# A decoder step on one Trainium2 core: two heads of the recurrent mixer share each level product

## The chip, the cores and the metric

One core of a Trainium2 chip runs the whole program. The metric is the device time of one execution in microseconds; the time before is a median of 2497.12 us over three runs.

## The reference

The program is one inference step of a two-layer decoder for a prompt of 1024 tokens and, with the same weights, for 8 sample tokens. Layer 0 mixes tokens with a gated linear recurrence (4 heads, a 128x128 state each) beside a memory attention; layer 1 with stick-breaking attention beside a memory attention; each layer ends in a SwiGLU FFN. The change concerns the recurrence of the prompt alone:

```python
b = jnp.cumsum(fi, axis=2)
o_inter = jnp.einsum('bhtk,bhkv->bhtv', qi * jnp.exp(b), S)
rel = b[:, :, :, None, :] - b[:, :, None, :, :]
dec = jnp.exp(jnp.where(causal, rel, -jnp.inf))
att = jnp.einsum('bhtk,bhsk,bhtsk->bhts', qi, ki, dec)
o = o_inter + jnp.einsum('bhts,bhsv->bhtv', att, vi)
```

The score of a query t and an earlier key s is a product over 128 features in which each feature has decayed by its own forget factors between s and t.

## The kernel before

The prompt is worked on in two halves of 512 tokens, g = 0 and g = 1; the sample's 8 tokens ride as columns 512 to 519 of the second half. Activations are feature-major: 128 features on the partitions, tokens along the columns. Weight products (`proj`, L274) split each fp32 weight into two parts (ACT L260, DVE L261) and multiply three times. The file is a set of generators; `weave` draws from several in turn, and the tile framework's scheduler then writes out a fixed order for each engine, by priority and by modelled times, so pieces of one generator may move past those of another. Engines wait for each other by semaphores, in order.

The recurrence of one half is `hgrn_prompt`. Its inputs, one pair of heads (`hp`) to a tile of [128, 2, 520], are forget factors F, keys K and queries Q from `gate_proj` and `heads2`, and the values V, token-major, from `v_proj`. For chunks of 128 tokens it builds the decayed score matrix `atts[h]` by doubling:

- The diagonal first: K times Q (L1160), masked by the identity (L1162); then Q is multiplied by F (L1167).
- Seven levels, m = 1, 2, ..., 64. A block of 2m tokens has an early and a late half of m tokens. All keys of a chunk are the stationary operand and the late queries the 64 moving columns (L1180): 8 fp32 matmuls for a pair of heads. Then DVE brings operands to the next level: late queries times the early half's total decay (L1185), early keys times the late half's total decay (L1186), and the totals of the halves multiplied (L1187). The block scores, early keys against late queries, go from PSUM into `atts` under a byte mask (L1190). One yield for each level and pair.
- Each head's end: keys turned (L1201), states (L1207, L1220), outputs from scores and values (L1215) and from the state carried in (L1219), and a norm (L303, L1226, L1228).

Score tiles and other temporaries come from pool `B` (7 buffers), level products from `S` (3 PSUM banks).

Where it stands in the order of the program:

- Setup: byte masks, two POOL selections (L163, L166) and one DVE cast (L169) each; rows of x are normed (L366 to L371), transposed (L396) and split (L399, L400).
- g = 0: `rows_proj` makes the values (L1048; its PSUM is copied out at L1054 and L1055), then gates and queries (`fq`), then the recurrence woven with the memory keys and values: `mem_keys` (L812, L817 to L822) and `mem_values` (L839).
- g = 1: gates and queries are woven with the memory attention of g = 0, the values with the end of the output projection, the recurrence with the first part of the FFN of g = 0 (`f0.part(0)`: L274 with L291 to L295 and L703).

Of the kernel before, what the change touches and what calls it, by code (L numbers as in the profile page):

```python
# [18 lines left out]
P = 128  # L19
# [5 lines left out]
def tile_decoder(  # L25
# [46 lines left out]
    def nm(s):  # L72
        uid[0] += 1
        return f"{s}_{uid[0]}"
# [62 lines left out]
    make_identity(nc, ident)  # L137
    ones = const.tile([P, P], F32, name="ones")
    nc.vector.memset(ones, 1.0)
    epsb = const.tile([P, 1], F32, name="epsb")  # L140
    nc.vector.memset(epsb, EPS)
    trif = const.tile([P, P], F32, name="trif")
# [11 lines left out]
        compare_op=ALU.is_equal, fill=0.0, base=0, channel_multiplier=0,  # L154
    )

    mask = const.tile([P, 7, 64], U8, name="mask")
    for lv in range(7):
        m = 1 << lv
        nb = 64 // m  # L160
        mf = tpool.tile([P, nb, m], F32, tag="t", name=nm("mf"))
        src = ones[:, 0:64].rearrange("p (b m) -> p b m", m=m)
        nc.gpsimd.affine_select(  # L163
            mf, src, pattern=[[-2 * m, nb], [0, m]], compare_op=ALU.is_ge, fill=0.0, base=0, channel_multiplier=1
        )
        nc.gpsimd.affine_select(  # L166
            mf, mf, pattern=[[2 * m, nb], [0, m]], compare_op=ALU.is_ge, fill=0.0, base=m - 1, channel_multiplier=-1
        )
        nc.vector.tensor_copy(mask[:, lv, :], mf.rearrange("p b m -> p (b m)"))  # L169

    xsraw = const.tile([P, ND, NB], F32, name="xsraw")
    par = const.tile([P, P], F32, name="par")
# [107 lines left out]
    def split_to(dst, src):  # L280
        nc.scalar.copy(dst[0], src)  # L281
        nc.vector.tensor_sub(dst[1], src, dst[0].bitcast(F32))  # L282

    def silu(dst, ps, g):

# [771 lines left out]
    def v_proj(g, W, m0, xt, vt, vs):  # L1057
        vt.extend((C(), C()) if g else (A(), A()))
        if not g:
            yield from rows_proj(W, m0, xt, vt)  # L1060
            return
        for h in range(H):
            ps = proj(g, W, 0, ND, m0 + h * P, xt)
            t = T()
            nc.scalar.copy(sv(t, g), pv(ps, g))
            to_token(t, vt, h)
            if g:
                nc.vector.tensor_copy(vs[:, h, :], t[:, G : G + NB])
            yield

    def gate_proj(g, W, xt, Ft, Kt):
        n = NG[g]
        for h in range(H):
            if h % 2 == 0:
                Ft.append(A())
                Kt.append(A())
            ps = proj(g, W, 0, ND, 4 * P + h * P, xt)
            f = T()
            nc.scalar.copy(sv(f, g), pv(ps, g))
            e = T()  # L1080
# [72 lines left out]
    def hgrn_prompt(g, Ft, Kt, Qt, Vt):  # L1153
        atts = []
        for h in range(H):
            K_, Q_ = Kt[h // 2][:, h % 2, :], Qt[h // 2][:, h % 2, :]
            pd = S()
            for c in range(CH):
                cs = slice(c * P, (c + 1) * P)
                nc.tensor.matmul(pd[:, cs], K_[:, cs], Q_[:, cs], start=True, stop=True)  # L1160
            at = B()
            nc.vector.tensor_mul(  # L1162
                at.rearrange("p (c t) -> p c t", c=CH), pd.rearrange("p (c t) -> p c t", c=CH),
                ident.unsqueeze(1).to_broadcast([P, CH, P]),
            )
            atts.append(at)
            nc.vector.tensor_mul(Q_[:, :G], Q_[:, :G], Ft[h // 2][:, h % 2, :G])  # L1167
            yield
        for lv in range(7):
            m = 1 << lv  # L1170
            nbg = G // (2 * m)
            for hp in range(2):
                F_, K_, Q_ = Ft[hp], Kt[hp], Qt[hp]
                pl = S()
                plv = pl.rearrange("p (h c n) -> p h c n", h=2, c=CH)
                for hh in range(2):
                    for c in range(CH):
                        cs = slice(c * P, (c + 1) * P)
                        rhs = Q_[:, hh, cs].rearrange("p (b t m) -> p b t m", t=2, m=m)[:, :, 1, :]
                        nc.tensor.matmul(plv[:, hh, c, :], K_[:, hh, cs], rhs, start=True, stop=True)  # L1180
                for hh in range(2):
                    Qv = Q_[:, hh, :G].rearrange("p (b t m) -> p b t m", t=2, m=m)
                    Kv = K_[:, hh, :G].rearrange("p (b t m) -> p b t m", t=2, m=m)
                    Fv = F_[:, hh, :G].rearrange("p (b t m) -> p b t m", t=2, m=m)
                    nc.vector.tensor_mul(Qv[:, :, 1, :], Qv[:, :, 1, :], Fv[:, :, 0, 0:1].to_broadcast([P, nbg, m]))  # L1185
                    nc.vector.tensor_mul(Kv[:, :, 0, :], Kv[:, :, 0, :], Fv[:, :, 1, 0:1].to_broadcast([P, nbg, m]))  # L1186
                    nc.vector.tensor_mul(Fv[:, :, 0, 0:1], Fv[:, :, 0, 0:1], Fv[:, :, 1, 0:1])  # L1187
                nb = 64 // m
                for hh in range(2):
                    nc.vector.copy_predicated(  # L1190
                        atts[hp * 2 + hh].rearrange("p (c b t m) -> p c b t m", c=CH, t=2, m=m)[:, :, :, 1, :],
                        mask[:, lv, :].rearrange("p (b m) -> p b m", m=m).unsqueeze(1).to_broadcast([P, CH, nb, m]),
                        pl[:, hh * 256 : (hh + 1) * 256].rearrange("p (c b m) -> p c b m", c=CH, m=m),
                    )
                yield
        for h in range(H):
            F_, K_, Q_ = Ft[h // 2][:, h % 2, :], Kt[h // 2][:, h % 2, :], Qt[h // 2][:, h % 2, :]
            pk = S()
            for c in range(CH):
                cs = slice(c * P, (c + 1) * P)  # L1200
                nc.tensor.transpose(pk[:, cs], K_[:, cs], ident)  # L1201
            kT = B()
            nc.scalar.copy(kT, pk)
            pd = S()
            for c in range(CH):
                cs = slice(c * P, (c + 1) * P)
# [3 lines left out]
            for c in range(CH):  # L1210
                cs = slice(c * P, (c + 1) * P)
                has = not (g == 0 and c == 0)
                cur = carry[:, h, :] if c == 0 else Sa[:, (c - 1) * P : c * P]
                nxt = carry[:, h, :] if c == CH - 1 else Sa[:, cs]
# [19 lines left out]
    class mixer_a:  # L1234
# [5 lines left out]

        def fq(self):
            yield from gate_proj(self.g, self.W, self.xt, self.F, self.K)
            yield from heads2(self.g, self.W, 0, self.xt, silu, A, self.Q)

        def v(self):
            yield from v_proj(self.g, self.W, 8 * P, self.xt, self.V, self.vs)
# [312 lines left out]
```

## Time and profile before

| | us |
|---|---|
| runs shown | 2499.96, 2497.12, 2493.58 |
| median | 2497.12 |
| the profiled execution | 2499.1 |
| its span, first to last instruction | 2497.4 |
| PE busy | 2462.8 |
| PEld (weight loads) busy | 2169.9 |
| DVE busy | 1571.8 |
| ACT busy | 1183.0 |
| POOL busy | 98.3 |

The granted TensorE clock is 0.997 over the span. The page gives busy time by engine and the chain of work that ended last; the trace can be asked for windows of time, for single lines of the code, for the instructions in order of time, and for waits. In a row of the timeline stand start and length in microseconds, the engine, the line, the operation, output and inputs, their sizes and the number of instructions; in brackets the idle time before it and what ended that. An fp32 matmul appears as two instructions.

### The profile page before, as it was taken

Reading aid. Unit: us, or ns where it says so; the run is one execution under the profiler, and the core shown is the slowest. Engines: PE = TensorE matmul, PEld = TensorE weight load, DVE = VectorE, ACT = ScalarE, POOL = GpSimd, SP = SyncE. Lnnn points to the kernel's source line nnn. Section 1 sums busy time; section 2 is a strip of 40 time slices with the busy share of each in tenths; the row PEclk is TensorE's granted clock in tenths of the full one; section 3 lists DMA queues with packets and bytes.
Section 4 is the critical chain, followed back from the end, with each engine's and each line's share of the span. In section 5 each row is a group of like instructions: output and inputs, shape, how many; then the busy total and the mean of one; then the engine's idle time right before and its main releaser. Section 6 shows DMA issues by size and latency. Waiting matters only on the chain.

```text
span 2497.4 us, 40764 instructions
## 1 busy us (share of the span) xinstructions
PE 2462.8 (99%) x15565; PEld 2169.9 (87%) x15565; DVE 1571.8 (63%) x2756; ACT 1183.0 (47%) x2277; POOL 98.3 (4%) x139
## 2 busy tenths in 40 slices
PE   8999999999999999999999999999999999999998
PEld 6888988877877897999999989877787797999997
DVE  5766556655765585655544575777577648755655
ACT  5446543243433454555433454555444445564444
POOL 1000000000000000010111100022000000000000
PEclk9999999999999999999999999999999999999999
DMA  5352252233643447586678976544454234365542
GB/s 186 114 165 68 72 156 81 60 110 116 184 124 98 129 138 227 156 195 177 173 191 215 234 193 196 160 142 138 121 149 130 85 115 122 121 192 145 151 137 69
DMA packets 496110, 358.21 MB, mean 143 GB/s; under 512 B 19110, under 2 KB 443635, under 8 KB 495915
## 3 DMA queue, kind: packets, MB, share of 16 engines
q1 hardware_dynamic: 477354, 301.08, 40.5%
q0 software_dynamic: 18560, 54.53, 9.1%
q8 instruction: 122, 2.00, 0.3%
q14 instruction: 74, 0.60, 0.1%
HBM read 325.73 MB, written 75.94 MB: 161 GB/s over the span
## 4 chain that ended last, share of the span: by engine, by line
PE 88%; DVE 5%; DMA 3%; ACT 2%; issue 2%; POOL 0%; SPq 0%; DVEq 0%; ACTq 0%; POOLq 0%
PE mm L274 59%; PE q L552 7%; PE q L667 5%; PE s L1180 2%; PE q L510 2%; PE mm L1048 2%; PE s L903 1%; PE s L862 1%; PE mm L812 1%; DMA b<-qd 1%; PE mm L839 1%; DVE ws L261 1%; PE ns L957 1%; PE s L1336 1%; DMA c<-in_cache_sb_v,pidx 1%
## 5 line engine op out<-in xcount | busy, mean ns | idle before, releaser
L274 PE MATMUL mm<-x,ws 128*128 128x260 f32 (+1 forms) x7776 | 1332.9, 330 | 0.0
L274 PEld LDWEIGHTS mm<-x,ws 128*128 128x128 f32 x7776 | 1148.3, 188 | 151.5 <-issue 12.0
L260 ACT CAST ws<-w 128x512 fp32r<-128x512 f32 x712 | 420.2, 591 | 763.2 <-PE mm L274 620.2
L261 DVE TENSOR_TENSOR ws<-w,ws 128x512 fp32r<-128x512 f32 x712 | 462.5, 653 | 286.8 <-ACT ws L260 278.3
L274 PE MATMUL mm<-m,ws 128*128 128x512 f32 (+1 forms) x2112 | 393.5, 343 | 0.1
L274 PEld LDWEIGHTS mm<-m,ws 128*128 128x128 f32 x2112 | 324.4, 189 | 49.9 <-issue 2.6
L667 PE MATMUL q<-m,ws 128*128 128x260 f32 x1056 | 128.8, 283 | 0.0
L667 PEld LDWEIGHTS q<-m,ws 128*128 128x128 f32 x1056 | 127.2, 188 | 0.4 <-ACT hT L485 0.2
L543 DVE TENSOR_TENSOR ws<-w,ws 128x512 fp32r<-128x512 f32 x126 | 86.6, 691 | 61.5 <-ACT ws L542 59.3
L552 PE MATMUL q<-y,ws 128*128 128x260 f32 x864 | 112.9, 283 | 0.0
L542 ACT CAST ws<-w 128x512 fp32r<-128x512 f32 x126 | 78.0, 621 | 69.6 <-PE q L667 27.4
L552 PEld LDWEIGHTS q<-y,ws 128*128 128x128 f32 x864 | 107.6, 189 | 0.0
L291 DVE TENSOR_SCALAR t<-mm 128x512 f32<-128x512 f32 (+1 forms) x82 | 56.7, 692 | 79.6 <-PE mm L274 79.6
L447 DVE TENSOR_TENSOR r<-r,mm 128x512 f32<-128x512 f32 (+1 forms) x96 | 66.0, 688 | 61.1 <-PE mm L274 60.3
L703 DVE TENSOR_TENSOR t<-t,mm 128x512 f32<-128x512 f32 (+1 forms) x66 | 45.5, 690 | 74.2 <-PE mm L274 73.9
L295 DVE TENSOR_TENSOR t<-t,t 128x512 f32<-128x512 f32 (+1 forms) x66 | 45.8, 694 | 70.6 <-ACT t L294 70.6
L552 PE MATMUL q<-x,ws 128*128 128x260 f32 x648 | 86.3, 282 | 0.0
L552 PEld LDWEIGHTS q<-x,ws 128*128 128x128 f32 x648 | 81.3, 188 | 0.0
L314 DVE TENSOR_TENSOR st<-st,n 128x512 f32<-128x512 f32 (+1 forms) x98 | 67.1, 691 | 8.8 <-ACT n L313 7.0
L281 ACT CAST m<-t 128x512 fp32r<-128x512 f32 (+1 forms) x88 | 54.9, 624 | 18.1 <-DVE t L703 8.9
L282 DVE TENSOR_TENSOR m<-t,m 128x512 fp32r<-128x512 f32 (+1 forms) x88 | 61.0, 693 | 2.6 <-ACT m L281 1.4
L984 POOL DMA_INDIRECT c<-in_cache_sb_k,pidx x16 | 16.4, 1026 | 1170.5 <-ACT n L313 958.6
(339 smaller groups left out, 2557.9 us busy)
## 6 DMA issues: line engine op xcount, KB each, us to landing
w<-in_w_gu SPq DMA_DIRECT2D x334, 256.0 KB, 3.4
w<-in_w_down SPq DMA_DIRECT2D x160, 256.0 KB, 3.5
w<-in_w_in_a SPq DMA_DIRECT2D x80, 256.0 KB, 3.0
wsum<-in_w_gu POOLq DMA_DIRECT2D x18, 1024.0 KB, 9.5
w<-wsum SPq DMA_DIRECT2D x72, 256.0 KB, 3.8
w<-in_w_o SPq DMA_DIRECT2D x64, 256.0 KB, 2.8
wsum<-in_w_gu POOLq DMA_DIRECT2D x12, 1280.0 KB, 10.7
w<-in_w_mem_kv SPq DMA_DIRECT2D x32, 256.0 KB, 3.2
```

Source lines behind the costliest of these rows:

```text
L260: nc.scalar.copy(ws[:, 0, :n, :], raw[:, :n, :])
L261: nc.vector.tensor_sub(ws[:, 1, :n, :], raw[:, :n, :], ws[:, 0, :n, :].bitcast(F32))
L274: nc.tensor.matmul(ps[:, a, : PW[g]], wt, xt[k][:, xi, o : o + PW[g]], start=(k == 0 and wi == 0), stop=(k == nk - 1 and wi == 2),)
L281: nc.scalar.copy(dst[0], src)
L282: nc.vector.tensor_sub(dst[1], src, dst[0].bitcast(F32))
L291: nc.vector.tensor_scalar(sv(x, g), pv(ps, g), -44.0, None, op0=ALU.max)
L314: nc.vector.tensor_add(acc[:, :n], acc[:, :n], t[:, :n])
L447: nc.vector.tensor_add(dst, dst, pv(ps, g))
L542: nc.scalar.copy(w[:, 0, :], src)
L543: nc.vector.tensor_sub(w[:, 1, :], src, w[:, 0, :].bitcast(F32))
L552: nc.tensor.matmul(ps[:, :h], w[:, wj, k * P : (k + 1) * P], x[:, xi, :], start=(first and k == 0 and wi == 0), stop=(k == 3 and wi == 2), ...
L667: nc.tensor.matmul(pp[a][:, :h], wt, mids[k][:, xi, a * h : (a + 1) * h], start=(k == 0 and wi == 0), stop=(k == nf - 1 and wi == 2),)
```

## The change

Two heads of a pair share each level product. The odd heads' tokens are stored back to front in time, so that where the even head's late halves are odd blocks, the odd head's are even blocks. A combined key matrix takes the even blocks of the even head and the odd blocks of the odd head (the early halves of each); it meets, as one moving operand of 128 columns, the late queries of both heads. Half of each product's rows belong to the wrong head and are left out by the masks, which now exist for both sides.

- In `hgrn_prompt` three storage places, x (the combined keys), y (the other blocks) and z (next level's x), take turns; `move` brings them from one level to the next: an ACT copy of blocks from y to z, a DVE scaling from x to z, a DVE scaling from x to y. A first `move` builds x, with one more yield. z is a tile from `B`.
- Query scalings and totals are one DVE instruction for the pair.
- `put` and `rev` write odd heads reversed in `gate_proj` and in the new `silu_heads`, with the 8 sample columns apart. The values of odd heads are reversed with a flip matrix on PE in the first half and by a reversed ACT write in the second. The chunks of odd heads are walked backwards, and their output is written reversed.

```diff
+    flip = const.tile([P, P], F32, name="flip")
+    nc.gpsimd.affine_select(
+        flip, ones, pattern=[[1, P]], compare_op=ALU.is_equal, fill=0.0, base=1 - P, channel_multiplier=1
+    )
...
+        for side in range(2):
+            o = side * m
...
+            nc.vector.tensor_copy(mask[:, lv, side, :], mf.rearrange("p b m -> p (b m)"))
...
+    def rev(ap):
+        st, n = ap.ap[-1]
+        return bass.AP(ap.tensor, ap.offset + (n - 1) * st, [list(d) for d in ap.ap[:-1]] + [[-st, n]])
+
+    def put(dst, src, h, g, op):
+        n = NG[g]
+        if h % 2 == 0:
+            op(dst[:, :n], src[:, :n])
+            return
+        op(dst[:, :G], rev(src[:, :G]))
+        if g:
+            op(dst[:, G:n], src[:, G:n])
...
+    def silu_heads(dst, ps, g, h):
...
+        put(dst, x, h, g, lambda o, i: nc.scalar.activation(o, i, AF.Exp, scale=-1.0))
+        nc.scalar.activation(d, d, AF.Ln, bias=1.0)
+        nc.scalar.activation(d, d, AF.Exp, scale=-1.0)
+        put(dst, x, h, g, lambda o, i: nc.vector.tensor_mul(o, o, i))
...
+            odd = [t[:, :, :512].rearrange("p c (e o d) -> p c e o d", o=2, d=P)[:, :, :, 1] for t in vt]
+            pts = [S(), S()]
+            for c in range(CH):
+                r = CH - 1 - c
+                nc.tensor.matmul(
+                    pts[c // 2][:, (c % 2) * 256 : (c % 2) * 256 + 256], flip, odd[r // 2][:, r % 2],
+                    start=True, stop=True,
+                )
+            for i in range(2):
+                pt = pts[i].rearrange("p (c e d) -> p c e d", c=2, d=P)
+                for c in range(2):
+                    nc.any.tensor_copy(odd[i][:, c], pt[:, c])
...
-            nc.scalar.activation(Fd, e[:, :n], AF.Exp)
-            nc.scalar.activation(Kd, f[:, :n], AF.Exp)
+            put(Fd, e, h, g, lambda o, i: nc.scalar.activation(o, i, AF.Exp))
+            put(Kd, f, h, g, lambda o, i: nc.scalar.activation(o, i, AF.Exp))
...
+        def view(t, o, *dims):
+            return bass.AP(t.tensor, t.offset + o, [list(t.ap[0])] + [list(d) for d in dims])
+
+        def move(F_, x, y, z, m):
+            if m == 0:
+                keep, swap, fk = [0, [2, G // 2]], [1, [2, G // 2]], None
+            elif m == 64:
+                keep, swap = [0, [P, CH], [1, m]], [m, [P, CH], [1, m]]
+                fk, fs = [m, [P, CH], [0, m]], [WID, [P, CH], [0, m]]
+            else:
+                nq = G // (4 * m)
+                keep, swap = [0, [4 * m, nq], [3 * m, 2], [1, m]], [m, [4 * m, nq], [m, 2], [1, m]]
+                fk = [m, [4 * m, nq], [WID + m, 2], [0, m]]
+                fs = [WID, [4 * m, nq], [3 * m - WID, 2], [0, m]]
+            nc.scalar.copy(view(z, *swap), view(y, *swap))
+            if fk is None:
+                nc.vector.tensor_copy(view(z, *keep), view(x, *keep))
+                nc.vector.tensor_copy(view(y, *swap), view(x, *swap))
+                return
+            nc.vector.tensor_mul(view(z, *keep), view(x, *keep), view(F_, *fk))
+            nc.vector.tensor_mul(view(y, *swap), view(x, *swap), view(F_, *fs))
+
+        xs, zs = [Kt[hp][:, 0, :G] for hp in range(2)], [B() for _ in range(2)]
+        for hp in range(2):
+            move(Ft[hp], xs[hp], Kt[hp][:, 1, :G], zs[hp], 0)
+            xs[hp], zs[hp] = zs[hp][:, :], xs[hp]
+        yield
...
-                plv = pl.rearrange("p (h c n) -> p h c n", h=2, c=CH)
-                for hh in range(2):
-                    for c in range(CH):
-                        cs = slice(c * P, (c + 1) * P)
-                        rhs = Q_[:, hh, cs].rearrange("p (b t m) -> p b t m", t=2, m=m)[:, :, 1, :]
-                        nc.tensor.matmul(plv[:, hh, c, :], K_[:, hh, cs], rhs, start=True, stop=True)
...
-                    nc.vector.tensor_mul(Qv[:, :, 1, :], Qv[:, :, 1, :], Fv[:, :, 0, 0:1].to_broadcast([P, nbg, m]))
-                    nc.vector.tensor_mul(Kv[:, :, 0, :], Kv[:, :, 0, :], Fv[:, :, 1, 0:1].to_broadcast([P, nbg, m]))
-                    nc.vector.tensor_mul(Fv[:, :, 0, 0:1], Fv[:, :, 0, 0:1], Fv[:, :, 1, 0:1])
...
+                for c in range(CH):
+                    o = c * P
+                    nc.tensor.matmul(
+                        pl[:, o : o + P], x[:, o : o + P],
+                        view(Q_, o + m, [WID - m, 2], [2 * m, nb], [1, m]), start=True, stop=True,
+                    )
+                late = view(Q_, m, [WID - m, 2], [2 * m, nbg], [1, m])
+                nc.vector.tensor_mul(late, late, view(F_, 0, [WID + m, 2], [2 * m, nbg], [0, m]))
+                move(F_, x, Kt[hp][:, 1, :G], z, m)
+                xs[hp], zs[hp] = z, x
+                first = F_[:, :, :G].rearrange("p h (b t m) -> p h b t m", t=2, m=m)
+                nc.vector.tensor_mul(first[:, :, :, 0, 0], first[:, :, :, 0, 0], first[:, :, :, 1, 0])
...
+                c = CH - 1 - i if h % 2 else i
...
-            nc.vector.scalar_tensor_tensor(F_[:, :G], po, hgn, r, op0=ALU.mult, op1=ALU.mult)
+            o = F_[:, :G]
+            if h % 2:
+                o = rev(o)
+            nc.vector.scalar_tensor_tensor(o, po, hgn, r[:, :G], op0=ALU.mult, op1=ALU.mult)
```

More of the change, by code (lines that the diff above doesn't have):

```diff
@@ L155, in tile_decoder @@
     )
-    mask = const.tile([P, 7, 64], U8, name="mask")
+    mask = const.tile([P, 7, 2, 64], U8, name="mask")
     for lv in range(7):
@@ L160, in tile_decoder @@
         nb = 64 // m
[L161 to L169, printed above, removed]
+        for side in range(2):
+            o = side * m
+            mf = tpool.tile([P, nb, m], F32, tag="t", name=nm("mf"))
+            src = ones[:, 0:64].rearrange("p (b m) -> p b m", m=m)
+            nc.gpsimd.affine_select(
+                mf, src, pattern=[[-2 * m, nb], [0, m]], compare_op=ALU.is_ge, fill=0.0, base=-o,
+                channel_multiplier=1,
+            )
+            nc.gpsimd.affine_select(
+                mf, mf, pattern=[[2 * m, nb], [0, m]], compare_op=ALU.is_ge, fill=0.0, base=o + m - 1,
+                channel_multiplier=-1,
+            )
+            nc.vector.tensor_copy(mask[:, lv, side, :], mf.rearrange("p b m -> p (b m)"))
     xsraw = const.tile([P, ND, NB], F32, name="xsraw")
@@ L282, in split_to @@
         nc.vector.tensor_sub(dst[1], src, dst[0].bitcast(F32))
+    def rev(ap):
[10 more added lines that the diff above has]
+    def silu_heads(dst, ps, g, h):
+        n = NG[g]
+        x = T()
+        d = dst[:, :n]
+        nc.vector.tensor_scalar(sv(x, g), pv(ps, g), -44.0, None, op0=ALU.max)
+        put(dst, x, h, g, lambda o, i: nc.scalar.activation(o, i, AF.Exp, scale=-1.0))
+        nc.scalar.activation(d, d, AF.Ln, bias=1.0)
+        nc.scalar.activation(d, d, AF.Exp, scale=-1.0)
+        put(dst, x, h, g, lambda o, i: nc.vector.tensor_mul(o, o, i))
     def silu(dst, ps, g):
@@ L1060, in v_proj @@
             yield from rows_proj(W, m0, xt, vt)
+            odd = [t[:, :, :512].rearrange("p c (e o d) -> p c e o d", o=2, d=P)[:, :, :, 1] for t in vt]
[5 more added lines that the diff above has]
+                    start=True, stop=True,
+                )
+            for i in range(2):
[3 more added lines that the diff above has]
+            yield
             return
@@ L1064, in v_proj @@
             t = T()
[L1065 to L1068, printed above, removed]
+            n = NG[g]
+            if h % 2:
+                o = rev(t[:, :n].rearrange("p (a n) -> p a n", a=2))
+                o = bass.AP(o.tensor, o.offset + n // 2, [list(o.ap[0]), [-(n // 2), 2], list(o.ap[2])])
+                nc.scalar.copy(o, pv(ps, g))
+                to_token(t[:, NB:n], vt, h)
+                nc.vector.tensor_copy(vs[:, h, :], rev(t[:, :NB]))
+            else:
+                nc.scalar.copy(sv(t, g), pv(ps, g))
+                to_token(t, vt, h)
+                nc.vector.tensor_copy(vs[:, h, :], t[:, G:n])
             yield
@@ L1168, in hgrn_prompt @@
             yield
+        def view(t, o, *dims):
[6 more added lines that the diff above has]
+                fk, fs = [m, [P, CH], [0, m]], [WID, [P, CH], [0, m]]
+            else:
+                nq = G // (4 * m)
[9 more added lines that the diff above has]
+            nc.vector.tensor_mul(view(y, *swap), view(x, *swap), view(F_, *fs))
@@ L1169, in hgrn_prompt @@
+        xs, zs = [Kt[hp][:, 0, :G] for hp in range(2)], [B() for _ in range(2)]
+        for hp in range(2):
+            move(Ft[hp], xs[hp], Kt[hp][:, 1, :G], zs[hp], 0)
+            xs[hp], zs[hp] = zs[hp][:, :], xs[hp]
+        yield
         for lv in range(7):
             m = 1 << lv
-            nbg = G // (2 * m)
+            nb, nbg = 64 // m, G // (2 * m)
             for hp in range(2):
-                F_, K_, Q_ = Ft[hp], Kt[hp], Qt[hp]
+                F_, Q_ = Ft[hp][:, :, :], Qt[hp][:, :, :]
+                x, z = xs[hp], zs[hp]
@@ L1174, in hgrn_prompt @@
                 pl = S()
-                plv = pl.rearrange("p (h c n) -> p h c n", h=2, c=CH)
-                for hh in range(2):
-                    for c in range(CH):
-                        cs = slice(c * P, (c + 1) * P)
-                        rhs = Q_[:, hh, cs].rearrange("p (b t m) -> p b t m", t=2, m=m)[:, :, 1, :]
[L1180 to L1187, printed above, removed]
@@ L1188, in hgrn_prompt @@
-                nb = 64 // m
+                for c in range(CH):
[3 more added lines that the diff above has]
+                        view(Q_, o + m, [WID - m, 2], [2 * m, nb], [1, m]), start=True, stop=True,
+                    )
+                late = view(Q_, m, [WID - m, 2], [2 * m, nbg], [1, m])
+                nc.vector.tensor_mul(late, late, view(F_, 0, [WID + m, 2], [2 * m, nbg], [0, m]))
+                move(F_, x, Kt[hp][:, 1, :G], z, m)
@@ L1193, in hgrn_prompt @@
-                        pl[:, hh * 256 : (hh + 1) * 256].rearrange("p (c b m) -> p c b m", c=CH, m=m),
+                        atts[hp * 2 + hh].rearrange("p (c b t m) -> p c b t m", c=CH, t=2, m=m)[:, :, :, 1 - hh, :],
+                        mask[:, lv, hh, :].rearrange("p (b m) -> p b m", m=m).unsqueeze(1).to_broadcast([P, CH, nb, m]),
+                        pl.rearrange("p (c h b m) -> p c h b m", c=CH, h=2, m=m)[:, :, hh],
                     )
@@ L1209, in hgrn_prompt @@
             po = S()
-            for c in range(CH):
+            for i in range(CH):
+                c = CH - 1 - i if h % 2 else i
                 cs = slice(c * P, (c + 1) * P)
-                has = not (g == 0 and c == 0)
-                cur = carry[:, h, :] if c == 0 else Sa[:, (c - 1) * P : c * P]
-                nxt = carry[:, h, :] if c == CH - 1 else Sa[:, cs]
+                has = not (g == 0 and i == 0)
+                cur = carry[:, h, :] if i == 0 else Sa[:, (i - 1) * P : i * P]
+                nxt = carry[:, h, :] if i == CH - 1 else Sa[:, i * P : (i + 1) * P]
                 nc.tensor.matmul(
@@ L1227, in hgrn_prompt @@
             r = rstd_from(osq, G, 1.0 / P, kT, S)
-            nc.vector.scalar_tensor_tensor(F_[:, :G], po, hgn, r, op0=ALU.mult, op1=ALU.mult)
+            o = F_[:, :G]
+            if h % 2:
+                o = rev(o)
+            nc.vector.scalar_tensor_tensor(o, po, hgn, r[:, :G], op0=ALU.mult, op1=ALU.mult)
             yield
@@ L1242, in fq @@
             yield from gate_proj(self.g, self.W, self.xt, self.F, self.K)
-            yield from heads2(self.g, self.W, 0, self.xt, silu, A, self.Q)
+            for h in range(H):
+                if h % 2 == 0:
+                    self.Q.append(A())
+                ps = proj(self.g, self.W, 0, ND, h * P, self.xt)
+                silu_heads(self.Q[-1][:, h % 2, :], ps, self.g, h)
+                yield
         def v(self):
```

2 lines of the change are left out of this document (removed).

## The prediction

> **What bounds the kernel now.** First the page: the summary of the engines and the chain of work that ended last.
>
> ```profile
> span 2497.4 us, 40764 instructions
> PE 2462.8 (99%) x15565; PEld 2169.9 (87%) x15565; DVE 1571.8 (63%) x2756; ACT 1183.0 (47%) x2277; POOL 98.3 (4%) x139
> ...
> PE 88%; DVE 5%; DMA 3%; ACT 2%; issue 2%; POOL 0%; SPq 0%; DVEq 0%; ACTq 0%; POOLq 0%
> PE mm L274 59%; PE q L552 7%; PE q L667 5%; PE s L1180 2%; PE q L510 2%; PE mm L1048 2%; PE s L903 1%; PE s L862 1%; PE mm L812 1%; DMA b<-qd 1%; PE mm L839 1%; DVE ws L261 1%; PE ns L957 1%; PE s L1336 1%; DMA c<-in_cache_sb_v,pidx 1%
> ```
>
> PE is the bound: 99% busy, 88% of the chain, and L1180, the level products that the change halves, holds 2% of the chain by itself. Next the chain in order of time (start, length, what), where each piece is the time until the next one takes over, so it gives the true spacing of the matmuls.
>
> ```profile
> 5.94 0.21 ACT rr L370
> ...
> 23.23 17.39 PE mm L1048 x75
> 40.61 44.38 PE mm L274 x192
> ...
> 89.90 0.45 PE s L1160 x4
> 90.35 1.73 PE s L1180 x16
> ...
> 112.06 1.73 PE s L1180 x16
> 113.80 2.82 PE mm L839 x12
> ...
> 430.17 4.41 PE s L1180 x40
> ...
> 501.57 0.88 PE s L303 x2
> ```
>
> One step of the level loop (one level, one pair of heads) is 8 fp32 matmuls of 64 moving columns; the trace has two instructions for each fp32 matmul, so x16, and they take 1.73 us: 108 ns an instruction. L1160 has the same stationary size and 128 moving columns: 0.45 / 4 = 112 ns. Twice the columns cost nearly nothing; the spacing goes by instructions.
>
> Third, where the loop runs, and what the other engines do there: the windows of L1180 alone (PE, PEld), then of all engines (PE, PEld, DVE, ACT, POOL, granted clock).
>
> ```profile
> 85.00:163.00 78.00, 27.38 (x224) 27.22 (x224) 1.00 0.48 145
> 416.00:490.00 74.00, 25.88 (x224) 26.17 (x224) 1.00 0.19 54
> ```
>
> ```profile
> 85.00:163.00 78.00, 77.31 (x576) 72.46 (x576) 67.99 (x170) 27.46 (x52) 0.00 (x0) 1.00 0.48 145
> 85.00:118.00 33.00, 32.31 (x255) 30.64 (x254) 31.18 (x68) 13.69 (x28) 0.00 (x0) 1.00 0.39 119
> 118.00:163.00 45.00, 45.00 (x324) 41.82 (x323) 36.82 (x103) 13.77 (x24) 0.00 (x0) 1.00 0.54 164
> 412.00:490.00 78.00, 78.00 (x459) 68.21 (x458) 56.27 (x145) 23.34 (x42) 0.00 (x0) 1.00 0.19 55
> ```
>
> There are two stages of 14 steps each: the first half of the prompt at 85 to 163 us, between pieces of the memory keys and values, and the second at 416 to 490 us, between FFN matmuls. PE is full in both. DVE is the second engine, and in the first 33 us of the first stage it is as full as PE (31.18 of 33.00). That is where I look for what the saving runs into.
>
> **The change part by part.**
>
> *Level products.* 28 steps fall from 16 to 8 instructions. At 112 ns a step costs 0.90 us where it cost 1.73: 0.83 us each, 11.6 us a stage, 23.2 us of PE time. This is the whole gain; the rest is cost.
>
> That the new moving operand has 128 columns picked with a stride is not in the trace: L1160's are contiguous, L1180's are strided, but with 64 columns a slowdown up to twofold would be under the spacing. Bounds for the new instruction are therefore 108 ns and 2 x 108 = 216 ns (nothing gained). I take 112, the row with the same column count. [...]
>
> *DVE in a step.* One step of the first stage before, at block size m = 8, and two back-to-back operations of 512 columns:
>
> ```profile
> 88.89 0.68 DVE L1162 TENSOR_TENSOR b<-s,ident 128x512 f32<-128x512 f32 x1
> 89.48 0.68 DVE L1167 TENSOR_TENSOR a<-a,a 128x512 f32<-128x512 f32 x1
> ...
> 126.64 0.42 DVE L1185 TENSOR_TENSOR a<-a,a 128x256 f32<-128x256 f32 x1 [0.87 <-PE s L1180]
> 126.98 0.42 DVE L1186 TENSOR_TENSOR a<-a,a 128x256 f32<-128x256 f32 x1
> 127.32 0.21 DVE L1187 TENSOR_TENSOR a<-a 128x32 f32<-128x32 f32 x1
> 127.53 0.43 DVE L1185 TENSOR_TENSOR a<-a,a 128x256 f32<-128x256 f32 x1
> ...
> 128.33 0.77 DVE L1190 COPY_PREDICATED b<-mask,s 128x256 f32<-128x256 uint8 x2
> 129.00 1.35 DVE L261 TENSOR_TENSOR ws<-w,ws 128x512 fp32r<-128x512 f32 x2
> ```
>
> From start to start, 256 columns take 0.34 us, 512 take 0.59. Before the masked copies a step has 126.64 to 128.33 = 1.69 us: two query scalings, two key scalings, two small products. After: one query scaling of 512 (0.59), two key scalings of 256 (0.68) and one small product of both heads (some 0.2 at m = 8) = 1.47. The masked copies keep their count and size. For the other levels the small product is as wide as 256 columns a head (m = 1) or 4 (m = 64):
>
> ```profile
> L1187 DVE TENSOR_TENSOR a<-a 128x256 f32<-128x256 f32 x4 | 1.7, 420 | 0.0
> L1187 DVE TENSOR_TENSOR a<-a 128x4 f32<-128x4 f32 x4 | 0.6, 159 | 0.0
> ```
>
> Merging saves 0.1 to 0.35 us a step by these spacings, some 2.3 us over 14 steps. The first rearrangement of the keys adds, for each of two pairs, two DVE copies of 256 columns (4 x 0.34 = 1.3 us). Net DVE: 1 us less a stage.
>
> *ACT in a step.* Every step, and the first rearrangement, gains one ACT copy of 256 columns, by L817 below 0.37 us: 16 a stage, 6 us on an engine with 27.46 of 78 us used. It depends only on the previous step of the same pair, so it is due a whole step before DVE's second key scaling, which must wait for it (that scaling overwrites what the copy reads). Behind that DVE instruction stand the masked copies and the weight splits L261 and L836, and PE waits for those. I cost it at nothing because it is early; uncovered it is the rival of the slower side.
>
> ```profile
> L817 ACT COPY t<-mm 128x256 f32<-128x256 f32 x8 | 3.0, 372 | 6.5 <-PE mm L812 6.5
> ```
>
> ```profile
> ACT ws L260 <- PE mm L839: 11.8, 6, 2.6
> ACT ws L835 <- PE mm L839: 10.7, 5, 2.6
> DVE a L1185 <- PE s L1180: 9.1, 11, 0.9
> ```
>
> *First stage.* PE would need 77.3 - 11.6 = 65.7 us, DVE 68.0 - 1.0 = 67.0. DVE becomes the longer of the two, so at best the stage shrinks by 78 - 67 = 11.0. DVE was idle for 10.0 us, 9.1 of them in 11 waits for level products (last row above). If all the idle time stays, the stage takes 77.0 and the gain is 1.0. The product waited for is half as long now, so I let half of it stay: 72 us with rounding up for the crowded start, a gain of 6.
>
> *Second stage.* DVE 56.3 - 1 = 55.3 us against PE 78 - 11.6 = 66.4: PE stays the bound. At best 11.6. The steps run in six bursts here (such as the x40 at 430.17); if PE waits for DVE once in each, at the 0.9 us of the wait row, 6.2 is left. I take 10.5, since the FFN weights are split ahead and the chain shows no gap on PE around the bursts.
>
> *Turning the values of odd heads.* Four fp32 matmuls of 256 columns with the flip matrix, 8 instructions: between L1160's 112 ns (128 columns) and L303's 440 ns (512 columns) each, so 0.9 to 3.5 us; by columns 220 ns, 1.8 us. They read the copies of PSUM that end the row projection, but the L274 matmuls of the gates follow without a gap (40.61 above) and can go first. If nothing goes first, PE also waits for the copy of the second bank:
>
> ```profile
> 40.65 1.23 DVE L1055 COPY a<-mm 128x1024 f32<-128x1024 f32 x1 [1.46 <-PE mm L1048]
> ```
>
> so the upper end is 4.8 us. I take 1.8. The four copies back (256 columns, 0.37 us on ACT) lie under the 44 us of L274.
>
> *Reversed writes.* Odd heads are written back to front by the same ACT and DVE operations; in the second half the 8 sample columns become 6 ACT and 2 DVE instructions more, at some 0.2 us (L370), under PE. No row shows a reversed ACT read; even doubled, 20 operations of 0.6 us are spread over stages where PE is full. Zero.
>
> *Setup.* Seven more masks (two POOL selections and a DVE cast each) and the flip matrix. The chain runs through them:
>
> ```profile
> 8.46 0.51 POOL mf L163 x2
> ...
> 10.52 0.25 POOL mf L166
> ...
> 10.79 0.19 DVE mask L169
> ...
> 13.57 0.48 PE ns L396
> ```
>
> Four masks took 8.46 to 10.79, 0.58 us each, and DVE's row scalings for the first transposes come behind the casts. Seven more cost 4.1 us if nothing moves between them, 0 if the rows go first. I take 2.0, and PE is not yet full at that point, so all of it is late.
>
> **Sum.** 6 + 10.5 - 1.8 - 2.0 = 12.7 us less. The profiled execution took 2499.1 us (span 2497.4 and 1.7 around it): 2486.4. The median of the three runs shown is 2497.1, 2.0 below it, which gives 2484.4. I put 2485. The ends: 11 + 11.6 - 0.9 - 0 = 21.7 less (2477), and 1 + 6.2 - 4.8 - 4.1 = 1.7 more (2501).
>
> **Rivals.** *DVE takes the place of PE.* The first stage gains 1, the second 6.2, the small costs as taken: 3.4 us less, 2495. For it: 31.18 of 33.00 us of DVE in the first part. Against: from 118 us on DVE has 8 us free, and the second stage has 22.
>
> *The paired product doesn't halve the time.* If 128 strided columns run at 216 ns an instruction, the levels below m = 64 (24 of 28 steps) gain nothing: the gain of PE is 4 x 0.83 = 3.3, less 3.8 of costs: 2499. If only m = 1 and 2 suffer (8 steps, 6.6 us), 2492. Against: L1180 has one spacing at all strides. [...]
>
> *Slower: the ACT copy is late.* Place: the copy before DVE's second key scaling. ACT works in order and waits up to 2.6 us for PE to free a split weight (rows above); a copy queued behind such a wait holds DVE, which is the bound of the first stage. Price: 14 x 2.6 = 36 us on DVE's 67 makes that stage 103, 25 longer; with 10.5 gained later and 3.8 of costs the kernel is at 2515. It decides (slower by over 7.5 us) from some 10 of 14 steps on. Against: the copy is ready a step earlier, and ACT is idle for most of the stage.
>
> **How the numbers follow.** Forecast 0.56 (its own range 2477 to 2491); DVE in PE's place 0.17; product not halved 0.08; ACT late 0.14; a little better than every bound, because other work is rearranged, 0.05. A measurement of this kernel can tell about 0.3% (7.5 us) from no change. Faster by more: 0.56 + 0.05 + 0.06 of the second and third = 0.67; slower 0.14; the same 0.19. The range goes from 2475 to 2502.
>
> **What would show it.** L1180's successor at x8 a step and 0.90 us in the chain; both stages shorter, the first by about 6, the second by about 10; DVE in the first stage above 93% busy; first dense matmuls some 2 us later than 23.23; no DVE wait on the new ACT copy over 0.5 us. I am wrong if the product's instructions space at over 150 ns, if the waits before the new copy sum to more than 10 us, or if a stage without level products changes by more than 3 us.

## The result and the profile after

The changed kernel takes 2482.07 us (median of six runs, 2480.22 to 2485.09) against 2497.03 us for the kernel before (six runs, 2493.58 to 2499.96): a ratio of 0.9941, 95% interval 0.9928 to 0.9954, some 15 us less. The forecast was 2485.

The line numbers have moved. The level products are now L1256 (L1180 before), the ACT copy of `move` L1234, its DVE scalings L1239 and L1240 and, at the first rearrangement, its DVE copies L1236 and L1237, the query scaling L1261, the totals L1265, the masked copies L1267; the masks L169, L173 and the cast L177; the flip products L1096. L274 is L282, L839 is L870, L812 is L843, L427 is L458 and L1128 is L1179.

The page of the changed kernel, engines first:

```profile
span 2483.4 us, 40356 instructions
PE 2443.6 (98%) x15349; PEld 2148.6 (87%) x15349; DVE 1571.8 (63%) x2719; ACT 1196.1 (48%) x2317; POOL 103.3 (4%) x154
```

PE is still the bound. It has 216 instructions less (28 x 8 = 224 fewer in the levels, 8 more for the flip products) and 19.2 us less work; its idle time grew from 34.6 to 39.8 us. So the PE work left as it should, and some 5 us of new waiting came in. Where, the chain in order of time tells:

```profile
27.14 17.62 PE mm L1079 x76
...
46.38 1.76 PE s L1096 x8
...
90.93 0.70 DVE t L309
...
150.34 0.89 PE s L1256 x8
151.23 2.76 PE mm L870 x12
...
441.12 1.80 PE s L1256 x16
...
482.37 0.89 PE s L1256 x8
```

The dense run of the row projection begins at 27.14 us where it began at 23.23. The flip products cost 1.76 us. A step of the level loop costs 0.89 us in the first stage and 0.89 to 1.01 in the bursts of the second, where it cost 1.73 to 1.77, at m = 64 (the last row) as at the small strides.

For the stages I take three landmarks that both kernels have: the evacuation that ends the last query projection before the first stage (L291, now L309, in the chain at 85.02 and 90.93 us), the first residual transpose between the stages (L427, now L458), and the first product of the sample recurrence after the second. The rows give the shortest, median and longest duration, then first and last start. Before:

```profile
L427 PE MATMUL ns<-ident,ht x64: 270/273/333, 341.4 to 999.2; 128*128 128x128 f32 x64
```

```profile
L1128 PE MATMUL s<-c,b x16: 587/588/692, 528.1 to 603.1; 8*128 8x512 f32 x16
```

After:

```profile
L458 PE MATMUL ns<-ident,ht x64: 270/272/329, 340.2 to 986.6; 128*128 128x128 f32 x64
```

```profile
L1179 PE MATMUL s<-c,b x16: 587/587/692, 517.4 to 591.4; 8*128 8x512 f32 x16
```

| piece | before | after | change |
|---|---|---|---|
| start of the first stage | 85.02 | 90.93 | +5.9 |
| from there to the first residual transpose | 256.4 | 249.3 | -7.1 |
| from there to the first sample product | 186.7 | 177.2 | -9.5 |
| from there to the last sample product | 75.0 | 74.0 | -1.0 |
| the rest of the span | 1894.3 | 1892.0 | -2.3 |

The second stage gained more than the 9.5 of the table. In these rows (count, then busy us, mean ns of one) the changed kernel has ten more FFN matmuls between the same landmarks. Before, then after:

```profile
L274 PE MATMUL mm<-x,ws 128*128 128x512 f32 x243 | 57.8, 395 | 0.0
```

```profile
L282 PE MATMUL mm<-x,ws 128*128 128x512 f32 x253 | 60.1, 395 | 0.0
```

At the 0.23 us between two of them in the chain (11.09 for 48) they are 2.3 us that the kernel before does later, so 9.5 stands for some 11.8: the whole saving of that stage arrived. The next piece has ten fewer matmuls and gains only 1.0, at a granted clock of 0.98 for 1.00.

The first stage gained 7.1 of its 11.6, with the same matmuls on both sides but for the halved ones. What it lost shows in the windows (PE, PEld, DVE, ACT, POOL, granted clock) of the changed kernel:

```profile
90.93:167.81 76.88, 73.28 (x490) 66.68 (x489) 69.09 (x150) 40.25 (x83) 0.00 (x0) 0.98 0.57 171
92.00:96.00 4.00, 3.32 (x31) 3.16 (x28) 3.95 (x8) 2.31 (x6) 0.00 (x0) 1.00 0.28 68
96.00:100.00 4.00, 1.60 (x10) 0.99 (x9) 3.82 (x10) 1.84 (x6) 0.00 (x0) 1.00 0.00 0
100.00:104.00 4.00, 4.00 (x22) 4.00 (x22) 3.52 (x9) 2.00 (x6) 0.00 (x0) 0.58 0.00 0
```

The reader is to see a hole at the very start: PE is busy 1.60 of 4 us at 96 to 100 while DVE is full, and in the next 4 us PE is full but at a granted clock of 0.58. In the whole stage PE is idle 3.60 us (0.68 before), 2.9 more; at 0.58 the 4 us hold 1.7 us less work. Together 4.6, which is about the 11.6 saved less the 7.1 gained.

One step of that stage on DVE at m = 8, to be held against the rows of the prediction (its two key scalings are those of the next level, which the planner runs a step early, and cost the same):

```profile
137.22 0.68 DVE L1261 TENSOR_TENSOR a<-a,a 128x512 f32<-128x512 f32 x1
137.82 0.42 DVE L1267 COPY_PREDICATED b<-mask,s 128x256 f32<-128x256 uint8 x1
138.15 0.27 DVE L1265 TENSOR_TENSOR a<-a 128x64 f32<-128x64 f32 x1
138.32 0.43 DVE L1267 COPY_PREDICATED b<-mask,s 128x256 f32<-128x256 uint8 x1
138.66 0.42 DVE L1239 TENSOR_TENSOR a<-b,a 128x256 f32<-128x256 f32 x1
138.99 0.42 DVE L1240 TENSOR_TENSOR a<-b,a 128x256 f32<-128x256 f32 x1
139.33 0.68 DVE L269 TENSOR_TENSOR ws<-w,ws 128x512 fp32r<-128x512 f32 x1
```

From 137.22 to 139.33 it is 2.11 us with the masked copies, 1.44 without (0.33 and 0.34 of spacing for the two); the prediction had 1.47. No DVE instruction waits for the ACT copy.

### The profile page after: what moved, and what is told of

It is laid out like the page before. It is cut to its first block, busy times and chain, and to the rows that moved or that the text cites. A ratio compares the mean times of both kernels' runs of the same rounds, so it can differ in the third digit from the quotient of the medians.

```text
span 2483.4 us, 40356 instructions
## 1 busy us (share of the span) xinstructions
PE 2443.6 (98%) x15349; PEld 2148.6 (87%) x15349; DVE 1571.8 (63%) x2719; ACT 1196.1 (48%) x2317; POOL 103.3 (4%) x154
## 4 chain that ended last, share of the span: by engine, by line
PE 92%; DVE 4%; ACT 1%; DMA 1%; issue 1%; SPq 0%; POOL 0%; DVEq 0%; ACTq 0%
PE mm L282 63%; PE q L583 7%; PE q L698 5%; PE q L541 2%; PE mm L1079 2%; PE s L934 1%; PE s L1422 1%; PE s L893 1%; PE ns L988 1%; PE s L1461 1%; PE s L1256 1%; PE s L1449 1%; PE s L920 1%; DVE ws L269 1%; PE mm L843 1%
## 5 line engine op out<-in xcount | busy, mean ns | idle before, releaser
L282 PE MATMUL mm<-x,ws 128*128 128x260 f32 (+1 forms) x7776 | 1334.2, 330 | 0.0
L282 PEld LDWEIGHTS mm<-x,ws 128*128 128x128 f32 x7776 | 1147.9, 188 | 151.7 <-issue 12.0
L282 PE MATMUL mm<-m,ws 128*128 128x512 f32 (+1 forms) x2112 | 392.2, 342 | 0.0
L282 PEld LDWEIGHTS mm<-m,ws 128*128 128x128 f32 x2112 | 324.1, 188 | 50.1 <-issue 2.3
L322 DVE TENSOR_SCALAR t<-mm 128x512 f32<-128x512 f32 (+1 forms) x74 | 51.2, 692 | 66.3 <-PE mm L282 66.2
```

The costliest lines, as they stand in the source:

```text
L282: nc.tensor.matmul(ps[:, a, : PW[g]], wt, xt[k][:, xi, o : o + PW[g]], start=(k == 0 and wi == 0), stop=(k == nk - 1 and wi == 2),)
L322: nc.vector.tensor_scalar(sv(x, g), pv(ps, g), -44.0, None, op0=ALU.max)
```

## The experiments

Eleven more kernels follow. Times are medians of each; ratios are to the kernel before in runs on the same chip, so they are what is compared.

### The halved products alone

```diff
                 for c in range(CH):
                     o = c * P
-                    nc.tensor.matmul(
-                        pl[:, o : o + P], x[:, o : o + P],
-                        view(Q_, o + m, [WID - m, 2], [2 * m, nb], [1, m]), start=True, stop=True,
-                    )
+                    for hh in range(2):
+                        nc.tensor.matmul(
+                            pl[:, o + hh * 64 : o + hh * 64 + 64], x[:, o : o + P],
+                            view(Q_, o + m + hh * (WID - m), [2 * m, nb], [1, m]), start=True, stop=True,
+                        )
```

> The changed kernel, but each shared level product of 128 moving columns is issued as two of 64, the even head's and the odd head's, against the same combined keys: 16 instructions a step again, everything else as changed. Theory A (the gain is the halved count of loads and matmuls on PE): a step costs 1.73 us again instead of 0.89, up to 28 x 0.84 = 23 us more than 2482, less what the start of the first stage takes back by having PE busier: about 2502, slower than the kernel before by the setup (4 us) and the flip products (1.8 us). Rival (the gain comes from fewer and merged DVE instructions or from a changed order): it stays within 5 us of 2482.

Measured: 2506.96 us, ratio 1.0034 (1.0021 to 1.0047). A step in its chain costs 1.73 to 1.76 us:

```profile
442.53 1.73 PE s L1257 x16
...
482.19 3.52 PE s L1257 x32
```

The whole gain, and 10 us more, is gone with the count of instructions. The number of columns, the data and everything written for DVE and ACT are those of the changed kernel. Theory A stands; without the halving the change is a loss of 0.3%. It is 5 us more than the 2502 expected: the products did not fill the start of the first stage, where PE is busy 2.09 of 4 us at 96 to 100 and 3.32 in the 4 us after.

### The setup's masks on POOL

```diff
-            nc.vector.tensor_copy(mask[:, lv, side, :], mf.rearrange("p b m -> p (b m)"))
+            nc.gpsimd.tensor_copy(mask[:, lv, side, :], mf.rearrange("p b m -> p (b m)"))
```

> The changed kernel with the 14 mask casts on POOL instead of DVE, so that DVE's row scalings no longer stand behind them. Theory A (the setup's delay passes to the end undiminished): the dense run of row-projection products starts at or before 23.2 us instead of 27.1, and the whole kernel is 4 to 6 us faster than the changed one, about 2477. Rival (the delay is made up for later, or the rows wait for something else such as the input loads): start or end moves by less than 2 us.

Measured: 2476.08 us, ratio 0.9913 (0.9899 to 0.9926). Its chain has the dense run at 22.18 us, and the first stage starts at 85.74:

```profile
22.18 17.39 PE mm L1079 x75
...
85.74 0.70 DVE t L309
```

The setup's delay goes to the end undiminished. In the changed kernel the chain walks through the POOL selections and DVE casts one by one, with DVE's row scalings behind them in its order:

```profile
8.46 0.12 DVE mask L177
8.64 0.76 POOL mf L169 x2
...
12.71 0.22 POOL mf L173
12.96 0.42 DVE mask L177 x2
...
13.53 1.25 DVE c L397
```

The same edit in the kernel before, with its 7 masks:

> The kernel before with its 7 mask casts on POOL. It tells which part of the setup's delay belongs to the change. Theory A (in the changed kernel the 7 added masks hold the row scalings some 4 us, the 7 old ones held them about 1): the dense run of row-projection products starts near 22.2 us instead of 23.2, and the kernel is some 1 us faster than before, 2496. Rival (the old masks already cost as much as the new ones): 3 us or more faster, 2494 or less.

Measured: 2496.87 us, ratio 0.9995 (0.9985 to 1.0004), dense run at 22.89 where it was at 23.23. The cost of the old masks can't be told from nothing; the new ones cost the 4 us.

### The start of the first stage

```diff
-    drain(a0.v(), a0.fq())
+    drain(a0.v())
+    weave((a0.fq(), 8), (mem_load(), 4))
     weave(
         (a0.core(), 22),
-        (chain(mem_load(), mem_keys(0), ...
+        (chain(mem_keys(0), ...
```

> The changed kernel with the memory tokens loaded and split (mem_load) beside the gate and query projections instead of beside the first steps of the recurrence. Theory A (in the first stage the changed kernel loses 2.9 us of PE idle time and some 1.7 us of a halved PE clock between 96 and 104 us, because DVE has the memory tokens' splits, the diagonals and the first rearrangement to do at once): PE is full there, the granted clock stays at 1.0 and the kernel takes 3 to 5 us less than the changed one, about 2478. Rival (the loss comes from DVE over the whole stage): the idle time moves to a later place of the stage and less than 2 us is gained.

Measured: 2476.48 us, ratio 0.9918 (0.9905 to 0.9932). The windows that had the hole:

```profile
92.00:96.00 4.00, 4.00 (x34) 3.92 (x33) 3.24 (x6) 3.03 (x5) 0.00 (x0) 1.00 0.40 121
96.00:100.00 4.00, 4.00 (x37) 4.00 (x36) 3.31 (x6) 1.51 (x3) 0.00 (x0) 1.00 0.50 133
100.00:104.00 4.00, 4.00 (x37) 4.00 (x36) 2.96 (x6) 1.51 (x3) 0.00 (x0) 1.00 0.70 197
```

PE is full and the clock is 1.00. The loss was at that place and not spread over the stage. A smaller edit at the same place puts all three copies of the first rearrangement on ACT:

```diff
-                nc.vector.tensor_copy(view(z, *keep), view(x, *keep))
-                nc.vector.tensor_copy(view(y, *swap), view(x, *swap))
+                nc.scalar.copy(view(z, *keep), view(x, *keep))
+                nc.scalar.copy(view(y, *swap), view(x, *swap))
```

> The changed kernel with all three copies of the first rearrangement on ACT instead of one on ACT and two on DVE. If DVE's extra 4 copies (some 0.9 us) are what opens the gap on PE at 96 to 100 us, the gap shrinks by about 1 us, and the clock may stay at 1.0 (1.7 us more). If the gap comes from the first products having to wait behind the diagonals of all heads, it stays within 0.5 us.

Measured: 2480.57 us, ratio 0.9929 (0.9914 to 0.9944), which can't be told from the changed kernel's by the times. Its windows:

```profile
96.00:100.00 4.00, 2.09 (x17) 1.68 (x15) 3.83 (x8) 1.80 (x6) 0.00 (x0) 1.00 0.02 4
100.00:104.00 4.00, 3.94 (x31) 3.55 (x30) 3.94 (x9) 3.24 (x10) 0.00 (x0) 1.00 0.00 0
```

The hole is 0.5 us smaller: DVE's four copies are the smaller part of it. The clock stays up, but it does so in two other kernels that by 102 us have left PE as idle as the changed kernel (3.10 us from 94 on, for 3.08; last section), so that is not put down to the edit. The rest, as far as the traces tell, is that PE has lost its filler: before, the products of the first level followed the diagonals at 90.35 us, needing nothing from DVE but Q times F; now they wait for the rearrangement, which ends on DVE at 99.9 us for the first pair, and the planner puts them at 111 us, behind memory keys whose operands DVE has still to split. With the copies on ACT one step's products start at 100.0, right behind the rearrangement, and PE is nearly full from there; the hole lies ahead of it. That the lost filler is the reason is argued from the traces; an order with the rearrangement ahead of the diagonals was not tried.

### DVE's room in the two stages

```diff
             nc.vector.tensor_mul(view(y, *swap), view(x, *swap), view(F_, *fs))
+            if g == 0:
+                nc.vector.tensor_mul(view(y, *swap), view(x, *swap), view(F_, *fs))
```

> The changed kernel with DVE's second key scaling (x to y, 256 columns) written twice at the levels of the first half of the prompt only; the repeat gives the same numbers and 14 more DVE instructions, some 5 to 6 us of DVE time. Theory A (after its crowded start the first stage is bound by PE, and DVE has little room: 3.67 us a step of PE against some 3.4 to 4.1 of DVE): a part of it shows, 2 to 5 us slower than the changed kernel, about 2485. Rival (DVE bounds the whole stage): all of it shows, 5 us or more. Other rival (PE bounds it with room to spare): less than 1 us.

Measured: 2485.70 us, ratio 0.9946 (0.9929 to 0.9962). From L309 to L458 its profile has 251.3 us (91.43 to 342.7), 2.0 more than the changed kernel, although its clock stayed at 1.00 after the hole, which by itself saves 1.7: so 3.7 of some 5 us of DVE work show. With `g == 1`:

> The same repeat at the levels of the second half only. Theory A (DVE is 79% busy there, PE is full): within 1.5 us of the changed kernel, 2482. Rival (DVE's backlog after each burst of level products holds PE in this stage too): 3 to 5 us slower.

Measured: 2482.75 us, ratio 0.9935 (0.9919 to 0.9952). From L458 to L1179 it takes 177.2 us (340.3 to 517.5), exactly as without the repeat. And without the scaling at all in the first half (`if g == 1:` ahead of the line; x is then not brought to y, and the scores of that half are not the reference's):

> The changed kernel without the second key scaling at the levels of the first half (x is not brought to y, so the first half's scores are not the reference's): 14 DVE instructions less, some 5 us of DVE time. Theory A: 0 to 3 us faster than the changed kernel, as PE bounds most of the stage. Rival (DVE bounds the stage): 4 us or more faster, about 2477.

Measured: 2481.65 us, ratio 0.9931 (0.9915 to 0.9948); from L309 to L458 248.6 us (90.72 to 339.3), 0.7 less. In the second stage DVE has room. In the first it sits at the edge: taking 5 us away gives 0.7, which is no more than two profiles of one kernel may differ by, and adding 5 costs 3.7. The rival that DVE bounds that whole stage falls.

### Both edits, and a further one

> The mask casts on POOL and the memory tokens beside the gate and query projections, both in the changed kernel. Theory A (two separate losses, one in the setup and one at the start of the first stage, which add): 6.0 + 5.6 = 11.6 us less than 2482.07, about 2470.5. Rival (the second is made up for when the first is gone, or they share a cause): 2475 or more.

Measured: 2471.88 us, ratio 0.9893 (0.9876 to 0.9909). The two losses are separate and add (10.2 us less than the changed kernel, where 11.6 was expected, within the intervals); this is the fastest version. The same two edits in the kernel before:

> The kernel before with both edits of the best version so far: mask casts on POOL and the memory tokens beside the gate and query projections. Theory A (the gap at the start of the first stage is the changed kernel's own, since before it PE had the first level's products to fill that time): 1 to 2.5 us faster than before, about 2496, and the change is worth some 24 us between kernels with both edits. Rival (the early memory tokens help either kernel alike): 5 us or more faster than before, 2491 or less.

Measured: 2497.47 us, ratio 0.9996 (0.9987 to 1.0005). They give nothing that shows there, so both losses are the change's own. Between kernels with both edits the change is worth 0.9996 - 0.9893 = 1.0% (some 26 us), of which 28 x 0.84 - 1.8 = 21.7 us are worked out from the steps and the flip products; the intervals (about 4 us each way) hold that.

In the fastest version PE still has a gap of 0.5 us in the second half of the first stage, at the end of this piece of its chain:

```profile
124.47 1.81 DVE ws L269 x3
126.28 0.34 DVE t L853
...
126.64 0.39 SPq L854
...
127.08 3.44 DMA w<-in_w_mem_kv
```

A store of memory keys (L854) waits in SP's queue for DVE's copy, and weight loads stand behind it.

```diff
-            nc.sync.dma_start(mks[l][:, h, :], src[:, :NM])
+            nc.gpsimd.dma_start(mks[l][:, h, :], src[:, :NM])
...
-            nc.sync.dma_start(
+            nc.gpsimd.dma_start(
                 mk_prompt[l, 0, :, h, :].rearrange("(t p) d -> p t d", p=P),
```

> The version with both edits, and the stores of the memory keys issued from POOL's queue instead of SP's. Theory A (in SP's queue the weight loads stand behind stores that wait for DVE's copies, which opens the gap of 0.5 us on PE in the second half of the first stage): no gap there, less than 1.5 us gained against 2471.9. Rival (the loads are late because their buffers come free late): the gap stays.

Measured: 2475.59 us, ratio 0.9910 (0.9894 to 0.9925): not faster. The gap grew to 1.1 us, and the chain now shows a load that starts right after DVE and takes longer:

```profile
122.07 0.38 DVE b L1267
122.45 6.45 DMA w<-in_w_mem_kv
```

Theory A falls: taking the stores out of SP's queue did not bring the weights in time. Whether the buffers' release or the load's own duration (3.44 and 6.45 us here) rules is open; at half a microsecond it was left so.

## Why the prediction was right, point by point

- **PE as the bound, 0.83 us a step.** Right: 0.84, and the halving alone carries the gain (the split products give 25 us back).
- **The strided operand of 128 columns at 112 ns.** Right: 0.89 us for 8 instructions is 111 ns at m = 64, and no step in the chain is above 1.01 (126 ns). The rival of unhalved products is out.
- **Second stage, 10.5.** Right, a little low: 9.5 to the first sample product, with ten more FFN matmuls done by then, so some 11.8. PE is full through it (177.15 of 177.20 us); none of the six waits that the prediction feared came.
- **First stage, 6.** The size came out near (7.1), but by luck: the step behind it was wrong. The prediction let DVE keep half of its idle time in all steps and so hold PE through the stage. The runs show instead one hole at the start, and a clock of 0.58 over the 4 us after it; PE is full from 104 us on but for half a microsecond, and taking DVE work away gains 0.7. The sentence that failed is "I let half of it stay". The sign that went with it, DVE above 93% busy in the first stage, failed too: 69.09 of 76.88 us, 90%. The windows of the first 33 us, which the prediction read as fullness, had the real hint: the first level's products were what PE did while DVE was full, and the change takes them from there.
- **Flip products, 1.8.** Measured 1.76, with other work ahead of them as assumed.
- **Setup, 2.0.** Mis-sized: the dense run starts 3.9 us later, almost the upper bound of 4.1. DVE's order has 13 of the 14 casts ahead of the third of the four row scalings, which therefore comes late.
- **DVE and ACT in a step.** Right at m = 8 (1.44 for 1.47). At m = 1 each key scaling takes 0.55 us for the 0.34 reckoned, 0.8 us a stage that the prediction left out. The ACT copy held no DVE instruction, as assumed; the rival of the slower side did not happen.
- **DVE in PE's place.** Fell with the runs that repeat or drop a key scaling, but near: the first stage has no room left on DVE.
- **Stages without level products** differ by 2.3 us in the two profiles, under the 3 us that would have spoken against the reading. It is not explained. Single profiles of one and the same setup begin their dense run anywhere from 26.69 to 28.14 us, so a microsecond or two between two profiles is no effect.
- **The sum.** The forecast of 2485 starts from the median of the runs, but the ends (2477 and 2501) and the rivals at 2495 and 2499 start from the profiled execution, which is 2.0 us longer. On one base they lie 2 us lower; no choice turns on it. That 2485 came within 3 us of 2482 is in part luck: 1.9 too little for the setup stands against 1.1 too little for the first stage and 2.3 us that no part of the change explains.

## What to carry to other kernels

Where two rows of the trace with the same stationary size and different columns show small matmuls spaced by the instruction and not by their columns (here 108 ns at 64 columns, 112 at 128), look for two that can be paired into one: here a step went from 1.73 to 0.89 us. Before work is taken off a full engine, look for what that work was covering: here the removed products had, by all the traces tell, filled PE while DVE was busy (before, at 90 to 94 us, PE for 4.00 of 4 us and DVE for 3.75). And count the setup: with seven more casts on DVE, in whose order the first real work also stands, the dense run began 3.9 us later, and with all 14 on POOL, 4% busy in the changed kernel, the time was 6.0 us less.

## What the runs showed of the hardware

The hole at the start of the first stage cost twice. After it the granted clock was 0.54 for 3.7 us (100.5 to 104.2 us, 0.50 from 101 to 104). By that clock it is 1.7 us of work not done (3.7 x 0.46), beside the 2.9 us by which PE was idle longer than before: from 100 to 104 us PE worked on 22 matmul instructions, where with the memory tokens early it worked on 37 at a clock of 1.00. How empty the hole was does not by itself decide it. With the scaling repeated in the second half PE was idle for 2.76 of the 6 us from 94 to 100, and the clock was 0.57 over the next 4; with the scaling repeated in the first half it was idle for 2.80 in the same window, and the clock stayed at 1.00. The clock also fell in the changed kernel (idle for 3.08, then 0.58) and without the scaling in the first half (2.90, then 0.57), and with the masks on POOL, where the hole lies some 5 us earlier (0.50 at 96 to 98). It stayed at 1.00 with the halved products split again (2.60) and with the copies on ACT (2.59). By 102 us the split products and the scaling repeated in the first half had each left PE idle for 3.10 us, still at 1.00. What decides between them the runs don't show. In the changed kernel's hole PE was idle for at most 1.45 us at a stretch (to 97.71 us).

Single elements at uneven steps took DVE longer here. At m = 1 the key scalings of the changed kernel read and write single elements whose steps alternate between 3 and 1. They take 0.55 us from start to start, where those at larger m take 0.32 to 0.40:

```profile
100.80 0.65 DVE L1239 TENSOR_TENSOR a<-b,a 128x256 f32<-128x256 f32 x1
101.36 0.64 DVE L1240 TENSOR_TENSOR a<-b,a 128x256 f32<-128x256 f32 x1
101.91 0.64 DVE L1239 TENSOR_TENSOR a<-b,a 128x256 f32<-128x256 f32 x1
```

Single elements alone are not the reason: the kernel before also scales single elements at m = 1, evenly two apart, and needs 0.34 us to the next start:

```profile
94.57 0.42 DVE L1186 TENSOR_TENSOR a<-a,a 128x256 f32<-128x256 f32 x1
94.91 0.42 DVE L1187 TENSOR_TENSOR a<-a 128x256 f32<-128x256 f32 x1
```

Whether the uneven steps of the keys or those of the factors cost the time was not separated.
